# A decoder layer in fp32 on one core: conditioning loaded as columns, and the order of products and low parts in the opening

## The chip, the cores and the metric

The kernel runs on one core of one Trainium2 chip. The core has five engines with queues of their own: TensorE (PE; its weight loads are listed as PEld), VectorE (DVE), ScalarE (ACT), GpSimd (POOL) and SyncE (SP, which here only issues DMAs); POOL issues DMAs too. Both kinds of issue are served by the core's 16 DMA engines. The metric is the device time of one execution in microseconds, as the median of several runs.

## The reference

One layer over 2048 tokens of width 1024, all in float32. A conditioning vector `c` gives six modulation rows; shift and scale act on each sub-layer's input, the gate on its output.

```python
cond = jax.nn.silu(c)
mod = (cond @ w_ada[l] + b_ada[l])[:, None, :]
sh1, sc1, g1, sh2, sc2, g2 = jnp.split(mod, N_MOD, axis=-1)
h = x * (1.0 + sc1) + sh1
z = h @ w_in[l]
gate_b, gate_c, v_conv, v_pool = jnp.split(z, [CONV_CH, 2 * CONV_CH, 3 * CONV_CH], axis=-1)
y_conv = gate_b * _short_conv(gate_c * v_conv, conv_w[l])
y_pool = _multiscale_pool(v_pool, w_pool[l], pool_scale[l])
mix = jnp.concatenate([y_conv, y_pool], axis=-1) @ w_out[l]
x = _layer_norm(DEEPNORM_ALPHA * x + (1.0 + g1) * mix, ln1_g[l], ln1_b[l])
h = x * (1.0 + sc2) + sh2
f = jnp.square(jax.nn.relu(h @ w_mlp_in[l])) @ w_mlp_out[l]
x = _layer_norm(DEEPNORM_ALPHA * x + (1.0 + g2) * f, ln2_g[l], ln2_b[l])
```

## The kernel before

The tokens are processed in two blocks of 1024 (`T`), with channels on the 128 partitions, so that the width of 1024 is eight "inputs" of 128 channels (`KD` = 8). Every fp32 operand of a matmul is split into a high part, rounded to TensorE's one-pass fp32 format by a ScalarE copy or activation, and a low part, the difference, by a VectorE subtraction (`split`, lines 78 to 80). A product is three matmuls: high by high, weights' high by low, weights' low by high (`mm3`, lines 83 to 86). Larger matrix products are done in Strassen's manner with seven block products, whose block sums are made on VectorE beside them.

**Modulation.** `w_ada` is laid out so that a row of the modulation, 128 channels of one of the six vectors, is a tile of 128x1024 (`wada[f]`). VectorE multiplies the tile by `cond`, the silu of `c` repeated on all partitions, and sums along the row: one `scalar_tensor_tensor` with an accumulated output per channel group (line 168). A bias add for a few groups at once turns the accumulated columns into columns of `mod` (line 170). The small tile `vecs` (128x80) holds the biases and other per-channel constants as columns; 1 is added to the scale and gate biases on chip (line 148).

**The opening.** Lines 92 to 107: `c` is loaded in two halves, each broadcast to 128 partitions by SyncE, ScalarE takes the sigmoid, VectorE the product. `vecs` comes over POOL's queue. The first two rows of `wada` and half of input 0 are loaded in halves. TensorE runs `WARM` = 18 small matmuls on an identity (line 115). `ada_first` makes `mod` for input 0.

**The first group** (`first_group`, lines 324 to 354) computes the first quarter of the input projection's columns for block 0, with all eight PSUM banks open as accumulators, over the eight inputs `k` in turn. For each `k`: two rows of `wada`, a 128x512 slice of weights and the 128x1024 input are loaded through `in_turn`, which chains the DMAs' issue order on SyncE; the two row products and the bias give `mod` for this input; then the weights are split, and `make_a` makes the high part of x * scale + shift (line 193), the same in full precision in place (line 195 on ScalarE, or line 197 on VectorE for inputs 0 and 1), and the low part (line 198). 24 matmuls follow (line 353): 4 column tiles, 2 halves of the tokens, 3 products.

In this code an input's low parts are issued before the next input's two row products. The order of instructions on each engine is made by a scheduler from the program; `tc.issue_after(x)` makes what stands under it come after x on its engine. The engines run their queues in order and wait for each other through semaphores.

After the first group the other three quarters follow in `group_mm`, with convolution and pooling of the group just done on VectorE and ScalarE. Right after the first group, eight more rows of `wada` (the gate `g1`) are loaded and multiplied. `spread` (line 173) then transposes the eight columns of the gate into a row repeated on all partitions: eight transposes on TensorE of a column broadcast along the free dimension, into two PSUM banks, and two ScalarE copies. The output weights are multiplied by this row.

Of the kernel before, what the change touches and what calls it, by code (L numbers as in the profile page):

```python
# [27 lines left out]
WINDOWS = (2, 4, 8, 16)  # L28
HALO = 16
HALF_SUMS = (2, 2, 3, 3, 3, 3, 2, 0)  # L30
WARM = 18
WW = T + HALO

SC1, SH1 = 0, 1
G1 = 16
SC2, SH2 = 24, 25
G2 = 40
VB, VC, VP, VG, VBB = 0, 48, 60, 64, 72


@with_exitstack
def tile_hybrid_layer(ctx: ExitStack, tc: tile.TileContext, xT, x, c, wada, vec, win0, win,
                      wins, wpool, wout, wmix, w1, w2, rows, out):
    nc = tc.nc

# [26 lines left out]
    def t_ps():  # L72
        return mk(pp, [P, H], F32, "ps", 8)
# [4 lines left out]
    def split(src, hi, lo):  # L78
        high = nc.scalar.copy(hi, src)  # L79
        return high.ins, nc.vector.tensor_tensor(lo, src, hi.bitcast(F32), op=ALU.subtract).ins  # L80
# [8 lines left out]
        return nc.vector.tensor_tensor(out_, a, b_, op=op)  # L89


    vecs = cp.tile([P, 80], F32, name="vecs")
    cond = t_o(D)
    sig = t_o(D)
    halves = [slice(h * H, h * H + H) for h in range(2)]
    for hs in halves:
        nc.sync.dma_start(cond[:, hs], c[hs].partition_broadcast(P))
    first = [t_h(F32), t_h(F32)]
    nc.gpsimd.dma_start(vecs, vec)
    for i, f in enumerate((SC1, SH1)):  # L100
        for hs in halves:
            nc.sync.dma_start(first[i][:, hs], wada[f][:, hs])
    x0 = t_o()
    nc.sync.dma_start(x0[:, :H], xT[0, 0][:, :H])
    for hs in halves:
        nc.scalar.activation(sig[:, hs], cond[:, hs], AF.Sigmoid)
        nc.vector.tensor_tensor(cond[:, hs], cond[:, hs], sig[:, hs], op=ALU.mult)
# [29 lines left out]
    msum = tc.dram_tile([7, NG - 1, P, H], F32, name="msum")  # L137
    wosum = tc.dram_tile([2, 4, P, T], F32, name="wosum")

    def ada_first():  # L140
        for i in range(2):
            for h, hs in enumerate(halves):
                summed = nc.vector.scalar_tensor_tensor(
                    first[i][:, hs], first[i][:, hs], 1.0, cond[:, hs], op0=ALU.mult, op1=ALU.mult,
                    accum_out=part[:, 2 * h + i : 2 * h + i + 1])
        with tc.issue_after(summed.ins):
            for a, b, s in ((SC1, 16, 2), (G1, 24, 1), (SC2, 40, 2), (G2, 48, 1)):
                nc.vector.tensor_scalar_add(vecs[:, a:b:s], vecs[:, a:b:s], 1.0)
        nc.vector.tensor_tensor(part[:, 0:2], part[:, 0:2], vecs[:, 0:2], op=ALU.add)
        return nc.vector.tensor_tensor(mod[:, 0:2], part[:, 0:2], part[:, 2:4], op=ALU.add)  # L150

# [4 lines left out]
    def in_turn(dst, src):  # L156
        if before:
            with tc.issue_after(before.pop()):
                d = nc.sync.dma_start(dst, src)
        else:  # L160
            d = nc.sync.dma_start(dst, src)
        before.append(d.ins)

    def ada(f0, f1, load=nc.gpsimd.dma_start, tiles=lambda: t_h(F32)):
        for f in range(f0, f1):
            r = tiles()
            load(r, wada[f])
            nc.vector.scalar_tensor_tensor(r, r, 1.0, cond, op0=ALU.mult, op1=ALU.mult,  # L168
                                           accum_out=acc[:, f : f + 1])
        return nc.vector.tensor_tensor(mod[:, f0:f1], acc[:, f0:f1], vecs[:, f0:f1], op=ALU.add)  # L170


    def spread(dst, cols):
        for h, hs in enumerate(halves):
            ps = t_ps()
            for i in range(4):
                k = 4 * h + i
                nc.tensor.transpose(ps[:, i * P : i * P + P], cols[:, k : k + 1].to_broadcast([P, P]), ident)
            nc.scalar.copy(dst[:, hs], ps)

    def row(t, src):
        nc.sync.dma_start(t, src.partition_broadcast(P))
# [3 lines left out]
    lnb = cp.tile([P, KD], F32, name="lnb")  # L186


    def make_a(r, k, cs=slice(0, T), a=None, act=True):
        ahi, alo = a or (t_h(), t_h())  # L190
        sc = mod[:, 2 * k + SC1 : 2 * k + SC1 + 1]
        sh = mod[:, 2 * k + SH1 : 2 * k + SH1 + 1]
        nc.scalar.activation(ahi[:, cs], r[:, cs], AF.Identity, bias=sh, scale=sc)  # L193
        if act:
            nc.scalar.activation(r[:, cs], r[:, cs], AF.Identity, bias=sh, scale=sc)  # L195
        else:
            nc.vector.tensor_scalar(r[:, cs], r[:, cs], sc, sh, op0=ALU.mult, op1=ALU.add)  # L197
        nc.vector.tensor_tensor(alo[:, cs], r[:, cs], ahi[:, cs].bitcast(F32), op=ALU.subtract)  # L198
        return ahi, alo

    def load_m(src):
        r = t_r()
# [115 lines left out]
    def store_mixed(j, y, pt, u, v):  # L318
# [2 lines left out]
                                r.rearrange("p (a n) -> p a n", a=2))  # L321
        nc.gpsimd.dma_start(msum[6, j], v[:, :H])

    def first_group(A):
        ps = {}
        for k in range(KD):
            wr, wt = t_r(), t_w()
            if k == 0:
                done = ada_first()
                a, wcuts = x0, [slice(0, P), slice(P, H)]  # L330
                for cs in wcuts:
                    in_turn(wr[:, cs], win0[k][:, cs])
                in_turn(a[:, H:], xT[0, 0][:, H:])
            else:
                done = ada(2 * k, 2 * k + 2, in_turn)
                in_turn(wr[:, :H], win0[k])
                a, wcuts = t_o(), [slice(0, H)]
                in_turn(a, xT[0, k])
            opened.append(done.ins)
            with tc.issue_after(done.ins):  # L340
                pair = None
                for i in range(2):
                    for cs in wcuts[i : i + 1]:
                        split(wr[:, cs], wt[:, cs], wt[:, H + cs.start : H + cs.stop])
                    pair = make_a(a, k, halves[i], pair, k > 1)
                A.append(pair)
            for h, hs in enumerate(halves):
                for p in range(3):
                    for m in range(4):
                        if k == 0 and p == 0:  # L350
                            ps[m, h] = t_ps()
                        w = (H if p == 1 else 0) + m * P
                        nc.tensor.matmul(ps[m, h], wt[:, w : w + P], A[k][p // 2][:, hs],  # L353
                                         start=k == 0 and p == 0, stop=k == KD - 1 and p == 2)
        return ps
# [67 lines left out]
    def beside(j, m, g1):  # L423
        for what in plan.get((j, m), "").split():
            n = int(what[1:])
            if what[0] == "r":
                ada(n, n + 2)
            elif what[0] == "f":
                fold(n, g1)
            elif what[0] == "b":  # L430
                spread(g1, mod[:, G1 : G1 + KD])
# [576 lines left out]
    def down(b, F, g2, close):  # L1008
# [78 lines left out]
        for n, (i, hf) in enumerate(steps):  # L1087
            ops, _ = ready
            if n + 1 < len(steps):
                ready = operands(n + 1)  # L1090
            if b == 0 and n < 2:
                ada(G2 + 4 * n, G2 + 4 * n + 4, nc.sync.dma_start, lambda: t_o(D))
            if b == 0 and 2 <= n < 6:
                sum_x(n - 2, ready[1])
            if n == 5:
                next(later)
            if 5 <= n < 9:
                later.send(ready[1])
            if i in (4, 6) and hf == 1:
                rest[i] = saved(hi_ if i == 4 else lo_)  # L1100
                if i == 6:
                    close.turn()
            banks, new, then = table[i]
            matmuls(banks, ops, new, hf == 0, hf == 1, then, hf == 1 and i in (4, 5, 6))
            if b == 0 and n == 4:
                spread(g2, mod[:, G2 : G2 + KD])


    class Close:
# [98 lines left out]
def _lay(inputs):  # L1208
# [7 lines left out]
    def pairs(p, q):  # L1216
# [3 lines left out]
    bada = np.concatenate([pairs(vsc1, vsh1), vg1, pairs(vsc2, vsh2), vg2])  # L1220
    conv = a["conv_w"][0].reshape(3, NG, P).transpose(1, 0, 2).reshape(3 * NG, P)
    vec = np.concatenate([bada, conv, a["pool_scale"][0].reshape(NG, P),
                          a["ln1_g"][0].reshape(KD, P), a["ln1_b"][0].reshape(KD, P)]).T
    w = a["w_in"][0].reshape(KD, P, 4, NG, P)[:, :, [3, 1, 2, 0]]
    return {
        "xT": x.T.reshape(KD, P, NB, T).transpose(2, 0, 1, 3),
        "x": x,
        "c": a["c"][0],
        "wada": wada,
        "vec": vec,  # L1230
        "win0": w[:, :, :, 0].reshape(KD, P, 4 * P),
# [27 lines left out]
```

## Time and profile before

| | |
|---|---|
| median of 3 runs | 1751.06 us (1750.05 to 1752.57) |
| the profiled execution | 1750.36 us |
| its span, first to last instruction | 1748.4 us |
| granted TensorE clock | 0.998 |
| TensorE busy | 1730.1 us, 99% |
| VectorE busy | 1264.6 us, 72% |
| ScalarE busy | 861.4 us, 49% |
| POOL busy | 191.6 us, 11% |

A row of the timeline has the start in us from the start of the span, the busy time of the instructions merged in it, engine, source line, operation, output and inputs by the program's names with their shapes, the count, and in brackets how long the engine stood idle before and what released it. A tile's name has its pool's tag only (`h`, `o`, `w`, `r`), so that several uses share one. "SPq" rows are DMA issues on SyncE's queue. A group's row has busy time and mean duration, then the idle time before. A row of the waits has the engine, line and releaser, then the total in us, the count and the longest.

### The profile page before, as it was taken

The numbers are of one execution on the slowest core, as the hardware profiler recorded it, in microseconds if no ns is written. First come the engines' busy times: TensorE is split into PE (matmuls) and PEld (weight loads), VectorE is DVE, ScalarE is ACT, GpSimd is POOL, SyncE is SP. The second block draws the span as 40 slices with busy tenths as digits, with TensorE's granted clock in tenths as the row PEclk, the third lists the DMA queues.
The fourth block names the chain that finished last, engine by engine and source line by source line (L and its number), as shares of the span: only waits on it lengthen the run. The fifth ranks groups of instructions, "written<-read, shape, count | busy, mean of one in ns | idle before, by whom it ended". The sixth has DMA issues, their size and how long they took to land.

```text
span 1748.4 us, 21342 instructions
## 1 busy us (share of the span) xinstructions
PE 1730.1 (99%) x7692; PEld 1429.7 (82%) x7692; DVE 1264.6 (72%) x1624; ACT 861.4 (49%) x1168; POOL 191.6 (11%) x374
## 2 busy tenths in 40 slices
PE   8999999999999999999999999999999999999997
PEld 6788888888888888888888888888888888888886
DVE  6998697877777685669686789686565656465774
ACT  4423348555445555446573344775445564344452
POOL 0122211122232000000000000101000100000000
PEclk9999999999999999999999999999999999999999
DMA  9799868687888999778681366655433479577761
GB/s 368 302 338 348 315 231 293 253 317 296 324 323 304 351 412 339 281 267 292 211 271 69 119 222 213 219 198 208 145 132 145 154 266 375 193 252 263 256 238 61
DMA packets 137227, 444.22 MB, mean 254 GB/s; under 512 B 15633, under 2 KB 16401, under 8 KB 137121
## 3 DMA queue, kind: packets, MB, share of 16 engines
q1 hardware_dynamic: 95040, 293.38, 47.0%
q0 software_dynamic: 42080, 149.49, 22.5%
q8 instruction: 60, 0.98, 0.2%
q14 instruction: 47, 0.38, 0.1%
HBM read 308.06 MB, written 134.74 MB: 253 GB/s over the span
## 4 chain that ended last, share of the span: by engine, by line
PE 94%; DVE 2%; DMA 1%; ACT 1%; issue 0%; SPq 0%; DVEq 0%
PE ps L84 31%; PE ps L85 31%; PE ps L86 31%; DVE h L168 1%; PE ps L704 1%; DMA r<-in_w 1%; ACT h L193 1%; DVE h L198 1%; DMA o<-in_w 0%; DVE o L89 0%; PE ps L353 0%; DMA r<-in_win 0%; DVE w L80 0%; ACT o L195 0%; DVE o L197 0%
## 5 line engine op out<-in xcount | busy, mean ns | idle before, releaser
L84 PE MATMUL ps<-h,w 128*128 128x512 f32 x1312 | 510.2, 389 | 0.7 <-ACT o L916 0.4
L85 PE MATMUL ps<-h,w 128*128 128x512 f32 x1312 | 510.3, 389 | 0.0
L86 PE MATMUL ps<-h,w 128*128 128x512 f32 x1312 | 510.1, 389 | 0.0
L84 PE MATMUL ps<-h,h 128*128 128x512 f32 x1120 | 436.0, 389 | 0.0
L86 PE MATMUL ps<-h,h 128*128 128x512 f32 x1120 | 435.9, 389 | 0.0
L85 PE MATMUL ps<-h,h 128*128 128x512 f32 x1120 | 435.7, 389 | 0.0
L79 ACT CAST h<-r 128x1024 fp32r<-128x1024 f32 (+1 forms) x184 | 186.8, 1019 | 306.9 <-PE ps L85 204.8
L80 DVE TENSOR_TENSOR h<-r,h 128x1024 fp32r<-128x1024 f32 (+1 forms) x184 | 216.5, 1182 | 112.8 <-ACT h L79 112.4
L79 ACT CAST w<-r 128x1024 fp32r<-128x1024 f32 (+2 forms) x165 | 169.2, 1026 | 260.3 <-PE ps L85 241.2
L84 PEld LDWEIGHTS ps<-h,w 128*128 128x128 f32 x1312 | 246.0, 188 | 53.0 <-ACT o L916 0.8
L85 PEld LDWEIGHTS ps<-h,w 128*128 128x128 f32 x1312 | 246.3, 188 | 51.3 <-DVE h L80 0.5
L86 PEld LDWEIGHTS ps<-h,w 128*128 128x128 f32 x1312 | 246.3, 188 | 51.2
L80 DVE TENSOR_TENSOR w<-r,w 128x1024 fp32r<-128x1024 f32 (+2 forms) x165 | 196.3, 1190 | 109.1 <-ACT w L79 107.4
L86 PEld LDWEIGHTS ps<-h,h 128*128 128x128 f32 x1120 | 210.2, 188 | 43.7
L84 PEld LDWEIGHTS ps<-h,h 128*128 128x128 f32 x1120 | 210.2, 188 | 43.6
L85 PEld LDWEIGHTS ps<-h,h 128*128 128x128 f32 x1120 | 210.2, 188 | 43.4
L89 DVE TENSOR_TENSOR o<-o,o 128x1024 f32<-128x1024 f32 (+1 forms) x170 | 162.4, 959 | 60.3 <-DMA usum<-o 45.7
L89 DVE TENSOR_TENSOR o<-o,ps 128x512 f32<-128x512 f32 x156 | 105.6, 684 | 58.9 <-PE ps L86 58.1
L80 DVE TENSOR_TENSOR h<-w,h 128x1024 fp32r<-128x1024 f32 x112 | 136.7, 1221 | 3.6 <-ACT h L79 3.6
L79 ACT CAST h<-w 128x1024 fp32r<-128x1024 f32 x112 | 117.5, 1049 | 6.8 <-DMA w<-in_w 6.3
L929 POOL DMA_DIRECT2D usum<-o x112 | 59.7, 534 | 520.2 <-ACT o L926 233.5
L89 DVE TENSOR_TENSOR r<-r,r 128x1024 f32<-128x1024 f32 x60 | 73.4, 1223 | 18.7 <-DMA r<-in_w 16.0
(133 smaller groups left out, 1180.4 us busy)
## 6 DMA issues: line engine op xcount, KB each, us to landing
usum<-o POOLq DMA_DIRECT2D x112, 512.0 KB, 4.7
r<-usum SPq DMA_DIRECT2D x112, 512.0 KB, 4.9
w<-w2sum SPq DMA_DIRECT2D x64, 512.0 KB, 6.0
r<-in_w SPq DMA_DIRECT2D x60, 512.0 KB, 4.9
w<-in_w SPq DMA_DIRECT2D x48, 512.0 KB, 6.9
o<-in_w SPq DMA_DIRECT2D x72, 256.0 KB, 6.3
w2sum<-o POOLq DMA_DIRECT2D x64, 256.0 KB, 6.6
h<-in_wada SPq DMA_DIRECT2D x22, 512.0 KB, 9.1
```

Source lines behind the costliest of these rows:

```text
L79: high = nc.scalar.copy(hi, src)
L80: return high.ins, nc.vector.tensor_tensor(lo, src, hi.bitcast(F32), op=ALU.subtract).ins
L84: nc.tensor.matmul(ps, whi, xhi, start=first, stop=False, skip_group_check=goes_on)
L85: nc.tensor.matmul(ps, whi, xlo, start=False, stop=False, skip_group_check=goes_on)
L86: nc.tensor.matmul(ps, wlo, xhi, start=False, stop=last, skip_group_check=goes_on)
L89: return nc.vector.tensor_tensor(out_, a, b_, op=op)
L168: nc.vector.scalar_tensor_tensor(r, r, 1.0, cond, op0=ALU.mult, op1=ALU.mult, accum_out=acc[:, f : f + 1])
L193: nc.scalar.activation(ahi[:, cs], r[:, cs], AF.Identity, bias=sh, scale=sc)
L198: nc.vector.tensor_tensor(alo[:, cs], r[:, cs], ahi[:, cs].bitcast(F32), op=ALU.subtract)
L704: nc.tensor.transpose(ps[:, t * P : t * P + P], R[4 * h + t][:, k * P : k * P + P], ident)
L929: nc.gpsimd.dma_start(usum[g, i], r)
```

## The change

`c` becomes eight more columns of `vecs` (128x88), which is now the first load on SyncE's queue. The silu is taken on the 128x8 columns, the additions of 1 stand with it, and `spread` transposes them into two PSUM banks at once. The half-row products for input 0 read those banks; after input 0's high parts ScalarE copies them to `cond` for all later products. `WARM` is 7. In `first_group`, the loads of the next input are issued by the program before an input's low parts, and for inputs 1 to 6 the next input's first row product is placed ahead of the low parts and its second behind them. Input 0 keeps both products of input 1 behind its low parts. Full precision x * scale + shift is made on ScalarE for input 1 too; input 0 keeps VectorE for it.

```diff
-WARM = 18
+WARM = 7
...
-    vecs = cp.tile([P, 80], F32, name="vecs")
-    cond = t_o(D)
-    sig = t_o(D)
+    vecs = cp.tile([P, 88], F32, name="vecs")
+    nc.sync.dma_start(vecs, vec)
     halves = [slice(h * H, h * H + H) for h in range(2)]
-    for hs in halves:
-        nc.sync.dma_start(cond[:, hs], c[hs].partition_broadcast(P))
     first = [t_h(F32), t_h(F32)]
-    nc.gpsimd.dma_start(vecs, vec)
...
-    for hs in halves:
-        nc.scalar.activation(sig[:, hs], cond[:, hs], AF.Sigmoid)
-        nc.vector.tensor_tensor(cond[:, hs], cond[:, hs], sig[:, hs], op=ALU.mult)
+    silu = cp.tile([P, KD], F32, name="silu")
+    nc.scalar.activation(silu, vecs[:, VX : VX + KD], AF.Sigmoid)
+    tt(silu, silu, vecs[:, VX : VX + KD], ALU.mult)
+    for a, b, s in ((SC1, 16, 2), (G1, 24, 1), (SC2, 40, 2), (G2, 48, 1)):
+        nc.vector.tensor_scalar_add(vecs[:, a:b:s], vecs[:, a:b:s], 1.0)
...
+    def spread(cols):
+        banks = []
+        for h in range(2):
+            ps = t_ps()
+            for i in range(4):
+                k = 4 * h + i
+                nc.tensor.transpose(ps[:, i * P : i * P + P], cols[:, k : k + 1].to_broadcast([P, P]), ident)
+            banks.append(ps)
+        return banks
+
+    def row_of(dst, cols):
+        banks = spread(cols)
+        for h, hs in enumerate(halves):
+            nc.scalar.copy(dst[:, hs], banks[h])
+
+    cond_banks = spread(silu)
...
+    cond = t_o(D)
+
     def ada_first():
         for i in range(2):
             for h, hs in enumerate(halves):
-                summed = nc.vector.scalar_tensor_tensor(
-                    first[i][:, hs], first[i][:, hs], 1.0, cond[:, hs], op0=ALU.mult, op1=ALU.mult,
+                nc.vector.scalar_tensor_tensor(
+                    first[i][:, hs], first[i][:, hs], 1.0, cond_banks[h], op0=ALU.mult, op1=ALU.mult,
                     accum_out=part[:, 2 * h + i : 2 * h + i + 1])
-        with tc.issue_after(summed.ins):
-            for a, b, s in ((SC1, 16, 2), (G1, 24, 1), (SC2, 40, 2), (G2, 48, 1)):
-                nc.vector.tensor_scalar_add(vecs[:, a:b:s], vecs[:, a:b:s], 1.0)
...
+    def dot(f, r):
+        return nc.vector.scalar_tensor_tensor(r, r, 1.0, cond, op0=ALU.mult, op1=ALU.mult,
+                                              accum_out=acc[:, f : f + 1])
+
+    def biased(f0, f1):
+        return nc.vector.tensor_tensor(mod[:, f0:f1], acc[:, f0:f1], vecs[:, f0:f1], op=ALU.add)
...
+        wcuts = [slice(0, P), slice(P, H)], [slice(0, H)]
+        done = ada_first()
+        _, wr, a = loads(0)
+        for k in range(KD):
+            wt = t_w()
+            hi, lo = t_h(), t_h()
+            A.append((hi, lo))
             opened.append(done.ins)
             with tc.issue_after(done.ins):
-                pair = None
-                for i in range(2):
-                    for cs in wcuts[i : i + 1]:
-                        split(wr[:, cs], wt[:, cs], wt[:, H + cs.start : H + cs.stop])
-                    pair = make_a(a, k, halves[i], pair, k > 1)
-                A.append(pair)
+                for cs in wcuts[k > 0]:
+                    split(wr[:, cs], wt[:, cs], wt[:, H + cs.start : H + cs.stop])
+                for hs in halves:
+                    high = shifted(hi, a, k, hs)
+                    if k:
+                        shifted(a, a, k, hs)
+            if k + 1 < KD:
+                rows_, wr_n, a_n = loads(k + 1)
+            if k == 0:
+                with tc.issue_after(high.ins):
+                    for hs, bank in zip(halves, cond_banks):
+                        nc.scalar.copy(cond[:, hs], bank)
+            elif k + 1 < KD:
+                done = dot(2 * k + 2, rows_[0])
+            with tc.issue_after(done.ins):
+                for hs in halves:
+                    if k == 0:
+                        sc, sh = (mod[:, 2 * k + i : 2 * k + i + 1] for i in (SC1, SH1))
+                        nc.vector.tensor_scalar(a[:, hs], a[:, hs], sc, sh, op0=ALU.mult, op1=ALU.add)
+                    low = tt(lo[:, hs], a[:, hs], hi[:, hs].bitcast(F32), ALU.subtract)
+            if k + 1 < KD:
+                with tc.issue_after(low.ins):
+                    for i in range(k > 0, 2):
+                        dot(2 * k + 2 + i, rows_[i])
+                done = biased(2 * k + 2, 2 * k + 4)
+                wr, a = wr_n, a_n
```

`loads(k)` issues input k's two rows of `wada`, its weights and its input through `in_turn`, in the order of before. `shifted` is one ScalarE activation of x * scale + shift.

More of the change, by code (lines that the diff above doesn't have):

```diff
@@ L37, with tile_hybrid_layer @@
 G2 = 40
-VB, VC, VP, VG, VBB = 0, 48, 60, 64, 72
+VB, VC, VP, VG, VBB, VX = 0, 48, 60, 64, 72, 80
 @with_exitstack
-def tile_hybrid_layer(ctx: ExitStack, tc: tile.TileContext, xT, x, c, wada, vec, win0, win,
+def tile_hybrid_layer(ctx: ExitStack, tc: tile.TileContext, xT, x, wada, vec, win0, win,
                       wins, wpool, wout, wmix, w1, w2, rows, out):
@@ L167, in ada @@
             load(r, wada[f])
[L168 to L179, printed above, removed]
+            dot(f, r)
+        biased(f0, f1)
     def row(t, src):
@@ L186, in tile_hybrid_layer, with shifted @@
     lnb = cp.tile([P, KD], F32, name="lnb")
[L189 to L199, printed above, removed]
+    def shifted(dst, r, k, cs):
+        return nc.scalar.activation(dst[:, cs], r[:, cs], AF.Identity, bias=mod[:, 2 * k + SH1 : 2 * k + SH1 + 1],
+                                    scale=mod[:, 2 * k + SC1 : 2 * k + SC1 + 1])
     def load_m(src):
@@ L325, in first_group, with loads @@
         ps = {}
[L326 to L331, printed above, removed]
+        def loads(k):
+            rows_ = [t_h(F32) for _ in range(2 if k else 0)]
+            wr, a = t_r(), t_o() if k else x0
+            for i, r in enumerate(rows_):
+                in_turn(r, wada[2 * k + i])
+            if k:
+                in_turn(wr[:, :H], win0[k])
+                in_turn(a, xT[0, k])
+            else:
+                for cs in wcuts[0]:
@@ L332, in first_group @@
                     in_turn(wr[:, cs], win0[k][:, cs])
                 in_turn(a[:, H:], xT[0, 0][:, H:])
[L334 to L338, printed above, removed]
+            return rows_, wr, a
+        wcuts = [slice(0, P), slice(P, H)], [slice(0, H)]
[5 more added lines that the diff above has]
+            A.append((hi, lo))
@@ new lines, in first_group @@
+                for hs in halves:
+                    high = shifted(hi, a, k, hs)
+                    if k:
+                        shifted(a, a, k, hs)
[7 more added lines that the diff above has]
+                done = dot(2 * k + 2, rows_[0])
@@ L430, in beside @@
             elif what[0] == "b":
-                spread(g1, mod[:, G1 : G1 + KD])
+                row_of(g1, mod[:, G1 : G1 + KD])
             elif what[0] == "l":
@@ L1105, in down @@
             if b == 0 and n == 4:
-                spread(g2, mod[:, G2 : G2 + KD])
+                row_of(g2, mod[:, G2 : G2 + KD])
     class Close:
@@ L1222, in _lay @@
     vec = np.concatenate([bada, conv, a["pool_scale"][0].reshape(NG, P),
-                          a["ln1_g"][0].reshape(KD, P), a["ln1_b"][0].reshape(KD, P)]).T
+                          a["ln1_g"][0].reshape(KD, P), a["ln1_b"][0].reshape(KD, P),
+                          a["c"].reshape(KD, P)]).T
     w = a["w_in"][0].reshape(KD, P, 4, NG, P)[:, :, [3, 1, 2, 0]]
@@ L1227, in _lay @@
         "x": x,
-        "c": a["c"][0],
         "wada": wada,
```

## The prediction

> **What bounds the kernel now.** I read the page first, then who made TensorE wait, then the timeline of the opening, instruction by instruction.
>
> ```profile
> span 1748.4 us, 21342 instructions
> PE 1730.1 (99%) x7692; PEld 1429.7 (82%) x7692; DVE 1264.6 (72%) x1624; ACT 861.4 (49%) x1168; POOL 191.6 (11%) x374
> PE ps L353 <- ACT h L193: 4.0, 4, 2.1
> PE ps L115 <- POOL ident masks.py:199: 3.2, 1, 3.2
> 87.00:131.00 44.00, 44.00 (x196) 36.45 (x195) 40.95 (x73) 8.93 (x12) 9.39 (x16) 1.00 0.91 339
> ```
>
> TensorE is busy 99% of the span, and its only large waits are in the opening: for its first instruction and for L353, the first group's matmuls. A later window (span, PE, PEld, DVE, ACT, POOL, clock, DMA share, GB/s) has it busy 44.00 of 44.00 us while the DMA engines are at 0.91. So what the opening loses is lost for good, and what it gains should carry to the end.
>
> ```profile
> 0.74 0.86 SPq L97 DMA_DIRECT2D o<-in_c  x2
> 3.23 6.29 PE L115 MATMUL ps<-ident 128*128 128x128 f32 x36 [3.23 <-POOL ident masks.py:199]
> 4.41 0.63 ACT L106 ACTIVATE o<-o 128x512 f32<-128x512 f32 x1 [2.39 <-DMA o<-in_c]
> 6.78 0.69 DVE L107 TENSOR_TENSOR o<-o,o 128x512 f32<-128x512 f32 x1 [1.01 <-ACT o L106]
> 7.39 0.68 DVE L143 SCALAR_TENSOR_TENSOR h<-h,o 128x512 f32<-128x512 f32 x1
> 8.00 0.69 DVE L143 SCALAR_TENSOR_TENSOR h<-h,o 128x512 f32<-128x512 f32 x1
> 9.83 0.39 DVE L148 TENSOR_SCALAR vecs<-vecs 128x8 f32<-128x8 f32 x4
> 10.32 0.16 DVE L150 TENSOR_TENSOR mod<-small 128x2 f32<-128x2 f32 x1
> 10.38 0.51 ACT L79 CAST w<-r 128x384 fp32r<-128x384 f32 x1 [0.21 <-DMA r<-in_win]
> 10.79 1.52 ACT L193 ACTIVATE h<-o,mod 128x512 fp32r<-128x512 f32 x2
> 11.65 17.40 PE L353 MATMUL ps<-h,w 128*128 128x512 f32 x72 [2.13 <-ACT h L193]
> 16.42 0.16 DVE L170 TENSOR_TENSOR mod<-acc,vecs 128x2 f32<-128x2 f32 x1
> 17.49 5.33 PEld L353 LDWEIGHTS ps<-h,w 128*128 128x128 f32 x24 [0.50 <-ACT h L193]
> ```
>
> This is the start. The conditioning arrives broadcast, in two transfers that delay everything behind them: the second half is through sigmoid and product only at 7.4; then four half-row products (L143), the 1+ of the biases, the modulation `mod` of input 0 at 10.48, its high part on ScalarE from 10.79 (just after a weight cast that waited for its load), matmuls at 11.65. Input 1 reaches TensorE at 17.49.
>
> ```profile
> 28.43 0.16 DVE L170 TENSOR_TENSOR mod<-acc,vecs 128x2 f32<-128x2 f32 x1
> 28.51 0.69 DVE L80 TENSOR_TENSOR w<-r,w 128x512 fp32r<-128x512 f32 x1
> 28.63 1.52 ACT L193 ACTIVATE h<-o,mod 128x512 fp32r<-128x512 f32 x2 [2.74 <-DVE mod L170]
> 30.06 1.51 ACT L195 ACTIVATE o<-o,mod 128x512 f32<-128x512 f32 x2
> 30.89 1.40 DVE L198 TENSOR_TENSOR h<-o,h 128x512 fp32r<-128x512 f32 x2 [1.69 <-ACT o L195]
> 32.21 1.22 DVE L168 SCALAR_TENSOR_TENSOR h<-h,o 128x1024 f32<-128x1024 f32 x1
> 33.35 1.22 DVE L168 SCALAR_TENSOR_TENSOR h<-h,o 128x1024 f32<-128x1024 f32 x1
> 34.62 0.16 DVE L170 TENSOR_TENSOR mod<-acc,vecs 128x2 f32<-128x2 f32 x1
> 60.68 0.39 PE L84 MATMUL ps<-h,w 128*128 128x512 f32 x1
> 61.36 0.39 PE L84 MATMUL ps<-h,w 128*128 128x512 f32 x1
> ```
>
> This is the loop, one turn for each input. From `mod` to `mod` is 34.62 - 28.43 = 6.19 us: four passes on ScalarE, two low parts on VectorE (L198), two whole-row products for the next input (L168), bias. An input gives TensorE 24 matmuls; three start within 61.36 - 60.68 = 0.68 us, so 24 need 5.44. TensorE idles about 0.75 us per input because the VectorE-ScalarE loop is longer than its own work.
>
> **The loop.** In the changed kernel's instruction order, from input 1 on, the next input's first product stands between the weights' low part (L80) and the first low part. VectorE now idles 1.69 us there, and the product takes 1.22: it fits with some 0.4 to spare. Nothing is queued behind it that is needed sooner, for the low parts wait for ScalarE's second pair anyway. The chain loses one product, 33.35 - 32.21 = 1.14, and becomes 5.05: below TensorE's 5.44, which is the new period. From 17.49 to the next group's first matmul at 60.68 there are 43.19 us; seven turns at 5.44 are 38.1. **Gain 5.1.** If the product didn't fit and delayed the low parts by its whole length, this would be 0; were the loop still the bound at 5.6, it would be 4.0. More than 5.1 isn't to be had, since TensorE sets the end.
>
> Loads must keep this pace:
>
> ```profile
> 21.56 1.62 SPq L159 DMA_DIRECT2D h<-in_wada  x2
> 26.08 1.63 SPq L159 DMA_DIRECT2D h<-in_wada  x2
> 7.00:9.00 2.00, 2.00 (x18) 2.00 (x17) 2.00 (x6) 0.00 (x0) 0.00 (x0) 1.00 1.06 397
> 3.00:5.00 2.00, 1.76 (x8) 1.77 (x9) 0.02 (x1) 0.59 (x1) 0.18 (x1) 1.00 0.97 236
> ```
>
> SyncE's issues for successive inputs are 26.08 - 21.56 = 4.52 apart with the engines full, under 5.44; the changed kernel issues the same loads in the same order. Loads stay ahead.
>
> **The start.** Removed: two transfers of 256 KB of broadcast, two sigmoids and two products over 512 columns. While the broadcast ran, the engines moved 236 GB/s, later 397; 0.5 MB less is at least 1.3 us at 397. Added: `c` as eight columns of `vecs` (45 KB, moved from POOL's queue to the head of SyncE's), a sigmoid and a product on 128x8, eight transposes into two PSUM banks, two copies to `cond`; the 1+ moves ahead of it all; 18 warm-up matmuls become 7.
>
> ```profile
> o<-in_c SPq DMA_DIRECT2D x2, 256.0 KB, 4.3
> vecs<-in_vec POOLq DMA_DIRECT2D x1, 40.0 KB, 5.0
> DMA  0499999999999999999999999999999999999999
> 82.60 0.87 PE ps L178 x8
> L294 DVE TENSOR_TENSOR o<-o,ps 128x512 f32<-128x512 f32 x1 | 0.7, 683 | 0.0
> L143 DVE SCALAR_TENSOR_TENSOR h<-h,o 128x512 f32<-128x512 f32 x4 | 2.5, 686 | 0.0
> ```
>
> When `vecs` lands is not in the trace. The DMA slices (1.5 us each) show engines starting near 2.5, so 2.7 is the earliest; the first broadcast half, six times as large and at the same place, was used at 4.41; the old `vecs`, stuck behind it, took 5.0, which from 0.74 would be 5.7. I take 3.3, nearer the early end because only 45 KB move. Then the four 1+ (0.39) and a small product (0.16): 3.9. Eight transposes take 0.87 at 82 us; cold, going by 9 matmul rows in 1.77 us, 0.2 each: banks at 4.7 and 5.5. Four half products, 0.61 apart; reading one operand from PSUM costs nothing (683 against 686 ns): 4.8 to 7.2, and 0.4 for accumulator and sums, `mod` at 7.6. Their rows, 1 MB from 2.7 on at about 390 GB/s, land by 5.5, and input 0 and its weights by 7. So 10.48 becomes 7.6, and I take **2.8** for the start, a little off for semaphores. Bounds: 3.5 with `vecs` at 2.7; 1.3 if the loads come only 1.3 earlier; 0.6 with `vecs` at 5.7. From `mod` of input 0 to that of input 1 nothing gets longer: 6.10 us now, the same VectorE work after. The two copies (about 0.6 each) run on ScalarE behind input 0's high parts, before the cast of input 1's weights, which waits for its load now; without that cover they cost 1.2. The first matmuls into the two banks they free stand behind seventeen others (3.9 us), so TensorE doesn't wait.
>
> The warm-up is where I look for a loss. Matmul rows go from 9 in 3-5 us to 17 in 7-9 us: TensorE runs at half rate for some 4.5 us after it first works. In the changed kernel it first works at 3.9 and has 8 transposes and 14 rows, 4.4 us at 0.2; input 0 comes at about 8.7. If it is still at half rate there for 2 us, 1 is lost, of which 0.5 falls into the wait for input 1. I take 0.2, with 0 to 1. [...]
>
> **Sum.** 2.8 + 5.1 - 0.2 = 7.7 us. The profiled execution took 1750.36 (its span and 1.96 around it), 0.7 under the median of 1751.06; from the median, **1743.4**.
>
> **Does it carry?** The next thing that could be late is the gate row: eight more products, summed at
>
> ```profile
> 80.22 0.17 DVE L170 TENSOR_TENSOR mod<-acc,vecs 128x8 f32<-128x8 f32 x1
> 41.98 5.92 SPq L159 DMA_DIRECT2D h<-in_wada  x8
> ```
>
> and transposed on TensorE at 82.60 (above): 2.2 us of slack, 19.7 us after the first group's end. I laid the changed VectorE order from that end: the same eight products and convolution work, one weight split more before them and one fewer, 19.8 us; TensorE comes there 21.9 after it. Their eight loads are issued by 47.9 now and land some 9 us later (the broadcast's 1.3 us earlier in the changed kernel); they are needed up to 70. POOL has one load fewer ahead of its first store; that product, too, stands later on VectorE, and no matmul waits for it.
>
> **Rivals.** (1) Only the start gains: the early product delays the low parts and the turn stays 6.19. Against it: 1.69 idle against 1.22. 1751.1 - 2.8 + 0.2 = 1748.5. (2) Only the loop gains, because `vecs` lands as late as on POOL's queue (its 5.0 speaks for it; that it then queued behind 0.5 MB, against): 0.6 + 5.1, 1745.4. (3) The gain is given back at the gate row: DMA near full through 62 us and an earlier TensorE make the eight products late. Each us beyond 2 us of slack is lost; 4 late leaves 1747, all of it 1751. (4) Slower: with 7 warm-ups and gaps of about 0.5 us, TensorE stays at half rate through the first inputs. Each us of that loses half; from 16 us on (an input and a half) the loss passes 7.7 and the kernel is slower than before. Through four inputs, 24 matmuls each in 10.9 instead of 5.44, it loses 22: about 1765. Against it: the rate rose within 5 us of near-solid work before, and after the present gap of 2.1 us input 0's 24 matmuls were still through before 17.49, 5.8 us after the first.
>
> **How the numbers follow.** Forecast 0.76, (1) 0.06, (2) 0.08, (3) 0.06, (4) 0.04. What a measurement of this kernel can tell from no change is 0.2%, 3.5 us. The forecast, (2) and half of (3) are faster by more: 0.87. (1), at 2.6, and the other half of (3) are within it: 0.09. (4) is slower: 0.04. The forecast's own range is 1742 to 1745.5 (start 3.5 to 1.3, clock 0 to 1); up to 1747.6 takes in (2) and half of (3), and the lower end gets 0.5 more for the spread of the runs: 1741.5 to 1747.6.
>
> **What would show it.** First-group matmuls starting near 8.7 instead of 11.65; `mod` rows 5.4 apart or less; TensorE without a wait between inputs from input 1 on; the next group's first matmul near 53 instead of 60.68; the gate's transposes 21.9 after it. I am wrong if `vecs` lands past 4.4, if VectorE's low parts wait for the early product, if matmul rows of input 0 are 0.45 apart for long, or if a TensorE wait appears between 53 and 90.

## The result: slower by 1.06%

| | before | after |
|---|---|---|
| median | 1751.06 us (1750.05 to 1752.57) | 1770.05 us (1767.11 to 1771.85) |
| ratio, with 95% interval | | 1.0106 [1.0091, 1.0121] |
| profiled execution | 1750.36 us | 1771.85 us |
| its span | 1748.4 us | 1769.6 us |

The forecast was 1743.4, within 1741.5 to 1747.6. The time lies 22 us above the range, and on the other side of no change. The profiled execution of after is the slowest of its five runs, so the profiles differ by 21.5 us where the medians differ by 19.0.

The page of the changed kernel: span, busy times, and the chain that ended last by engine.

```profile
span 1769.6 us, 21316 instructions
PE 1752.8 (99%) x7678; PEld 1433.0 (81%) x7678; DVE 1264.6 (71%) x1621; ACT 862.1 (49%) x1171; POOL 191.1 (11%) x373
...
PE 92%; issue 2%; DMA 2%; DVE 2%; ACT 1%; SPq 0%; POOL 0%; DVEq 0%; ACTq 0%; POOLq 0%
```

TensorE is busy 99% of a longer span: 22.7 us more (1752.8 against 1730.1) with no more matmuls. VectorE, ScalarE and POOL are busy as long as they were, to within 1 us. So no wait took the place of another; TensorE itself works longer for the same matmuls. The groups of instructions, shapes kept apart (busy us, mean ns of one), say which, first after, then before:

```profile
L85 PE MATMUL ps<-h,w 128*128 128x512 f32 x1312 | 517.5, 395 | 0.0
L84 PE MATMUL ps<-h,w 128*128 128x512 f32 x1312 | 517.5, 395 | 1.2 <-DVE o L89 1.2
L84 PE MATMUL ps<-h,h 128*128 128x512 f32 x1120 | 436.0, 389 | 0.0
...
L387 PE MATMUL ps<-h,w 128*128 128x512 f32 x192 | 47.4, 410 | 2.6 <-ACT h L202 2.6
```

```profile
L85 PE MATMUL ps<-h,w 128*128 128x512 f32 x1312 | 510.3, 389 | 0.0
L84 PE MATMUL ps<-h,h 128*128 128x512 f32 x1120 | 436.0, 389 | 0.0
```

Matmuls with one operand in a tile `h` and the other in a tile `w` take 395 ns instead of 389; those with both in `h` take 389 in both kernels. That is no clock: the same instruction is slower or not by the tiles it reads. The windows (span, PE, PEld, DVE, ACT, POOL, clock, DMA share, GB/s) agree. Between 400 and 440 us the matmuls are of the first kind, between 640 and 680 of the second; after, then before:

```profile
400.00:440.00 40.00, 40.00 (x173) 32.17 (x172) 29.77 (x35) 18.48 (x22) 10.65 (x20) 1.00 0.81 302
640.00:680.00 40.00, 40.00 (x178) 33.11 (x178) 25.30 (x26) 20.46 (x21) 2.13 (x4) 1.00 1.01 397
```

```profile
400.00:440.00 40.00, 40.00 (x178) 33.13 (x177) 31.12 (x37) 18.36 (x22) 11.67 (x22) 1.00 0.85 324
```

In the same 40.00 us, with no idle time and the clock at 1.00, there are 173 matmuls instead of 178; in the other window 178. From start to start an `h,w` matmul takes 0.2328 us instead of 0.2268. Two rows of the timeline of after, twelve matmuls apart, show it: (60.63 - 57.84) / 12 = 0.2325.

```profile
57.84 0.39 PE L84 MATMUL ps<-h,w 128*128 128x512 f32 x1
...
60.63 0.39 PE L84 MATMUL ps<-h,w 128*128 128x512 f32 x1
```

Some 4110 such pairs at 6.0 ns make 24.6 us. Now the opening of after, by the timeline:

```profile
2.48 0.21 ACT L102 ACTIVATE silu<-vecs 128x8 f32<-128x8 f32 x1 [0.46 <-DMA vecs<-in_vec]
3.08 1.94 PE L118 MATMUL ps<-ident,silu 128*128 128x128 f32 x8 [3.08 <-DVE silu L89]
4.21 0.69 DVE L161 SCALAR_TENSOR_TENSOR h<-h,ps 128x512 f32<-128x512 f32 x1 [1.27 <-PE ps L118]
4.81 3.19 PE L131 MATMUL ps<-ident 128*128 128x128 f32 x14
7.23 0.69 DVE L161 SCALAR_TENSOR_TENSOR h<-h,ps 128x512 f32<-128x512 f32 x1 [2.32 <-DMA h<-in_wada]
8.83 0.30 ACT L79 CAST w<-r 128x128 fp32r<-128x128 f32 x1 [6.14 <-DMA r<-in_win]
9.24 0.16 DVE L165 TENSOR_TENSOR mod<-small 128x2 f32<-128x2 f32 x1
10.59 21.74 PE L387 MATMUL ps<-h,w 128*128 128x512 f32 x82 [2.58 <-ACT h L202]
...
20.38 0.16 DVE L184 TENSOR_TENSOR mod<-acc,vecs 128x2 f32<-128x2 f32 x1
22.84 1.40 DVE L89 TENSOR_TENSOR h<-o,h 128x512 fp32r<-128x512 f32 x2 [0.50 <-ACT o L202]
25.42 0.16 DVE L184 TENSOR_TENSOR mod<-acc,vecs 128x2 f32<-128x2 f32 x1
```

`vecs` lands at 2.48, earlier than forecast, but the second half-row product then waits 2.32 us for its row; `mod` is there at 9.40 (9.24 + 0.16) instead of 7.6, the first weights are cast only at 8.83, and the first matmul comes at 10.59 instead of 8.7. The loop does what was forecast: `mod` to `mod` is 25.42 - 20.38 = 5.04, and VectorE still idles 0.50 between the early product and the low parts.

Both kernels issue the same matmuls in the same order after the warm-up, so each can be set against itself. Start after minus start before, from the single records:

| point | after - before | what happened since the point above |
|---|---|---|
| first matmul of the first group | -1.1 us | the start gains 1.1 |
| first matmul of input 1 | +1.1 | 12 matmuls of input 0 some 427 ns apart, none before: 2.2 lost |
| first matmul of the next group (57.84 against 60.68) | -2.8 | -4.0: the loop gains 5.0, and gives back 1.0 to slower matmuls |
| end | +21.2 | some 23.4 from slower matmuls, and some 0.7 given back |

### The profile page after: what moved, and what is told of

Its sections match the earlier page's. It is cut to its first block, busy times and chain, and to the rows that moved or that the text cites. A ratio compares the mean times of both kernels' runs of the same rounds, so it can differ in the third digit from the quotient of the medians.

```text
span 1769.6 us, 21316 instructions
## 1 busy us (share of the span) xinstructions
PE 1752.8 (99%) x7678; PEld 1433.0 (81%) x7678; DVE 1264.6 (71%) x1621; ACT 862.1 (49%) x1171; POOL 191.1 (11%) x373
## 4 chain that ended last, share of the span: by engine, by line
PE 92%; issue 2%; DMA 2%; DVE 2%; ACT 1%; SPq 0%; POOL 0%; DVEq 0%; ACTq 0%; POOLq 0%
PE ps L84 30%; PE ps L85 30%; PE ps L86 30%; PE ps L387 3%; PE ps L738 1%; DMA w2sum<-o 0%; DVE h L80 0%; DVE o L89 0%; DMA usum<-o 0%; DMA r<-winsum 0%; DMA r<-in_xT 0%; DMA r<-in_win 0%; ACT h L587 0%; DMA r<-in_wins 0%; DMA r<-xsum 0%
## 5 line engine op out<-in xcount | busy, mean ns | idle before, releaser
L84 PE MATMUL ps<-h,w 128*128 128x512 f32 x1312 | 517.5, 395 | 1.2 <-DVE o L89 1.2
L86 PE MATMUL ps<-h,w 128*128 128x512 f32 x1312 | 517.7, 395 | 0.1
L85 PE MATMUL ps<-h,w 128*128 128x512 f32 x1312 | 517.5, 395 | 0.0
L84 PE MATMUL ps<-h,h 128*128 128x512 f32 x1120 | 436.0, 389 | 0.0
L86 PE MATMUL ps<-h,h 128*128 128x512 f32 x1120 | 435.9, 389 | 0.0
L79 ACT CAST w<-r 128x1024 fp32r<-128x1024 f32 (+2 forms) x165 | 168.9, 1024 | 296.4 <-PE ps L85 282.0
L84 PEld LDWEIGHTS ps<-h,w 128*128 128x128 f32 x1312 | 246.8, 188 | 60.0 <-DVE o L89 1.6
L86 PEld LDWEIGHTS ps<-h,w 128*128 128x128 f32 x1312 | 246.8, 188 | 59.0 <-DVE w L80 0.5
L80 DVE TENSOR_TENSOR h<-r,h 128x1024 fp32r<-128x1024 f32 (+1 forms) x184 | 216.0, 1179 | 107.9 <-ACT h L79 107.5
L80 DVE TENSOR_TENSOR w<-r,w 128x1024 fp32r<-128x1024 f32 (+2 forms) x165 | 196.2, 1189 | 126.2 <-ACT w L79 124.5
L86 PEld LDWEIGHTS ps<-h,h 128*128 128x128 f32 x1120 | 210.2, 188 | 43.8
L84 PEld LDWEIGHTS ps<-h,h 128*128 128x128 f32 x1120 | 210.3, 188 | 43.6
L80 DVE TENSOR_TENSOR h<-w,h 128x1024 fp32r<-128x1024 f32 x112 | 136.3, 1217 | 3.7 <-ACT h L79 3.7
```

The lines of the kernel that those rows point to most:

```text
L84: nc.tensor.matmul(ps, whi, xhi, start=first, stop=False, skip_group_check=goes_on)
L85: nc.tensor.matmul(ps, whi, xlo, start=False, stop=False, skip_group_check=goes_on)
L86: nc.tensor.matmul(ps, wlo, xhi, start=False, stop=last, skip_group_check=goes_on)
```

## The experiments

The theory for the 24.6 us: where the tiles lie in SBUF. Tiles of one tag get their place when the tag is first used. Before, `cond` and `sig` (tag `o`) came first, then `first` (tag `h`); the change allocates `first` ahead of any `o`. An `o` tile has 4160 bytes per partition (T + HALO numbers) and there are ten, 41600 bytes, which is no multiple of 256. They now lie between `h` and `w`. From the compiled programs, first byte of each tag in a partition:

```
kernel           order     h       o       w        w - h
before           o h r w   59776   18176   194944   135168 = 33 x 4096
after            h o r w   18240   132928  195008   176768 = 43 x 4096 + 640
before_h_first   h o r w   18176           194944   176768 = 43 x 4096 + 640
o_first          o h r w                            135168 = 33 x 4096
pad128           h o r w                            43 x 4096 + 768 = 691 x 256
pad64            h o r w                            43 x 4096 + 704 = 690 x 256 + 192
```

The rivals: something in the new order of the opening, or the shorter warm-up, slows the later matmuls. For what remains of the opening: the loop, the start, the warm-up, each alone.

**The place alone, in the changed kernel (o_first).** The tag `o` first again.

```diff
+    x0 = t_o()
     first = [t_h(F32), t_h(F32)]
...
-    x0 = t_o()
```

> The changed kernel with one allocation moved: the tile x0 (tag o) is made before the tiles of the first two rows (tag h), so that the tags stand in SBUF in the order o, h, r, w as before the change. Then w stands a multiple of 4096 bytes past h again (it is 640 more than one in the changed kernel). Theory of the addresses (weights and moving operand collide when they stand 640 bytes apart beyond multiples of 4096): the 4110 matmuls ps<-h,w take 227 ns from start to start again instead of 233, 24.6 us go, and the time is 1770 - 24.6 = 1745.5. Rival, the absolute place of w (448 past a multiple of 2048 instead of 384, which this edit leaves as it is): stays 1770. Rival, the PSUM banks taken in another turn, or the new order of instructions: stays 1770.

1747.28 us (1744.17 to 1751.33) against 1750.34: 0.9982 [0.9972, 0.9991]. A group of its matmuls, and its next group's first one:

```profile
L85 PE MATMUL ps<-h,w 128*128 128x512 f32 x1312 | 510.3, 389 | 0.0
```

```profile
55.66 0.39 PE L84 MATMUL ps<-h,w 128*128 128x512 f32 x1
```

One allocation moved, with the same work on each engine, is 22.8 us of medians, 1.8 less than was expected; the runs of this kernel spread over 7.2 us. The next group starts 5.0 us ahead of before.

**The place alone, in the kernel before (before_h_first).**

```diff
+    first = [t_h(F32), t_h(F32)]
     cond = t_o(D)
     sig = t_o(D)
...
-    first = [t_h(F32), t_h(F32)]
```

> The kernel before with the reverse edit and nothing of the change: the tiles of the first two rows are made before the conditioning's, so that the tags stand in the order h, o, r, w and w is 640 bytes more than a multiple of 4096 past h. Theory of the addresses: the matmuls ps<-h,w take 233 ns and the time is 1751 + 24.6 = 1775.6. Rivals (absolute place of w, PSUM banks, order of instructions): stays 1751.

1772.45 us (1772.13 to 1772.61) against 1750.34: 1.0125 [1.011, 1.014]. These 22.1 us are 2.5 fewer than the 24.6 expected. By the single records the slower matmuls cost 23.5 us behind the first group and nothing within it, where TensorE waits for the loop; the first group starts 0.4 us earlier, and two waits of TensorE near 341 and 353 us come out 1.0 us shorter. The old opening and the old order of products, with 395 ns:

```profile
L86 PE MATMUL ps<-h,w 128*128 128x512 f32 x1312 | 517.5, 395 | 0.0
```

The rivals fall: the loss needs nothing of the change but the order of allocation.

**The distance by itself (offsets).** Almost all of the layer is left out: 192 matmuls per source line, weights and moving operand at chosen distances in one tile.

```python
run(lambda *s, **k: mm(*s, **k), 0, 64)
...
run(lambda *s, **k: mm(*s, **k), 64, 64)
```

The first number is the moving operand's shift in bytes, the second the weights'.

> Matmuls alone, in the kernel's form (128x512 moving, 128x128 weights, high/low pattern of three), 192 for each distance between weights and moving operand, on the same data; almost all of the layer is left out. A line of the code for each distance: 0, 0, 16, 32, 64, 128, 192, 256, 320, 384, 448, 512, 640, 1024, 2048 bytes beyond multiples of 4096 with the moving operand at a multiple of 2048, then moving and weights both 64 past, moving alone 64 past, both 128 past, moving alone 128 past, both 32 past. Theory of the addresses: 389 ns mean duration at distance 0 and with both shifted together, about 395 at 640 and at 128; what 16 to 64 and 256, 512, 1024 and 2048 do is open, and tells the period of the collision. Rival, absolute place: both 64 past is slow, 640 (a multiple of 128) is not. Rival, neither: 389 on all lines.

Six of its groups; L72 is a distance of 0, L75 of 64, L76 of 128, L77 of 192, L78 of 256, and on L86 both operands are shifted by 64:

```profile
L72 PE MATMUL ps<-a 128*128 128x512 f32 x192 | 43.7, 389 | 0.0
L75 PE MATMUL ps<-a 128*128 128x512 f32 x192 | 45.0, 395 | 0.0
L76 PE MATMUL ps<-a 128*128 128x512 f32 x192 | 44.8, 395 | 0.0
L77 PE MATMUL ps<-a 128*128 128x512 f32 x192 | 44.1, 391 | 0.0
L78 PE MATMUL ps<-a 128*128 128x512 f32 x192 | 43.7, 389 | 0.0
L86 PE MATMUL ps<-a 128*128 128x512 f32 x192 | 43.7, 389 | 0.0
```

Of the other distances, 16, 512, 1024 and 2048 gave 389, 448 gave 391, and 32, 320, 384 and 640 gave 395. Shifting the moving operand alone gave 391 for 64 and 395 for 128; shifting both by 32 or 128 gave 389. So over the distances tried the pattern repeats every 256 bytes, and it is the distance between the two operands that counts, not the address of either.

**The distance in the changed kernel (pad128, pad64).** The order of allocation stays, with unused bytes between `o` and `w`.

```diff
     x0 = t_o()
+    big.tile([P, 32], F32, name="pad")
```

pad64 has 16 in place of 32.

> The changed kernel with its tags in its own order (h, o, r, w) and 128 unused bytes per partition between o and r, so that w stands 768 bytes past h beyond multiples of 4096, a multiple of 256. Theory of the addresses with a period of 256 (from the run of the distances): the matmuls ps<-h,w take 227 ns and the time is that of the kernel with the allocation moved, 1747. Rival, what counts is the order of the tags or the region of SBUF in which h lies: stays 1770.

> The same with 64 unused bytes: w stands 704 bytes past h, 192 beyond a multiple of 256. Theory of the addresses with a period of 256: the distance of 192 had 2.1 ns more for each matmul than 0 (44.1 against 43.7 us for 192), so 4110 matmuls lose 8.8 us and the time is 1747 + 9 = 1756. Rival, any distance off a multiple of 256 costs the same 6 ns: 1771.

pad128: 1746.67 us (1745.15 to 1749.12) against 1750.89, 0.9977 [0.9968, 0.9987]. pad64: 1754.69 (1752.27 to 1756.06), 1.0023 [1.0012, 1.0034]. 128 idle bytes are worth 23.4 us. 64 bytes, which leave 192 past a multiple of 256, are worth part of it; groups of pad64:

```profile
L85 PE MATMUL ps<-h,w 128*128 128x512 f32 x1312 | 515.1, 393 | 0.0
L86 PE MATMUL ps<-h,w 128*128 128x512 f32 x1312 | 510.1, 389 | 0.0
```

Two of the three products of `mm3` are slower there (L84 is 393 too) and the third isn't; by single records that is 8.9 us over the whole kernel.

**The loop alone (reorder_only).** The kernel before with the new `first_group`; conditioning, 18 warm-ups and places as before.

```diff
+            if 0 < k < KD - 1:
+                done = dot(2 * k + 2, rows_[0])
+            with tc.issue_after(done.ins):
+                for hs in halves:
...
+                    low = tt(lo[:, hs], a[:, hs], hi[:, hs].bitcast(F32), ALU.subtract)
```

> The kernel before with the new order in the first group alone (the next input's first product ahead of the low parts, full precision on ScalarE from input 1 on); conditioning, warm-up and places in SBUF as before. Theory of the loop: the chain from input to input is shorter than TensorE's 5.44 us, 5.1 us go in the opening, about 1 comes back at the stall near 350 us: 1750.3 - 4.1 = 1746.2. Rival, the loop's gain needs the early start: 1749 or more.

1745.65 us (1745.34 to 1746.35): 0.9972 [0.9962, 0.9982], 5.2 us under the kernel before on the same chip (1750.89). Its next group starts at 55.65 instead of 60.68:

```profile
55.65 0.39 PE L84 MATMUL ps<-h,w 128*128 128x512 f32 x1
```

**The columns alone (columns_only, columns_mended).** o_first with 18 warm-ups and the old `first_group`.

```diff
+                if k == 0:
                     for hs, bank in zip(halves, cond_banks):
                         nc.scalar.copy(cond[:, hs], bank)
```

> The changed kernel with the first group's order of before, 18 warm-up matmuls, and the tags in the order o, h, r, w: of the change only the conditioning as columns is left. Theory of the start: input 0's matmuls begin 1.5 us earlier, the loop of 6.19 us an input carries this on: 1750.3 - 1.5 = 1748.8. Rival, the loads of the first inputs set the pace of the loop when it starts earlier: no gain, 1750.3.

1750.04 us (1748.42 to 1752.42): 0.9997 [0.9987, 1.0006]. Its timeline says that it was no clean measure of the columns:

```profile
9.61 1.07 ACT L362 COPY o<-ps 128x512 f32<-128x512 f32 x2
10.57 1.53 ACT L205 ACTIVATE h<-o,mod 128x512 fp32r<-128x512 f32 x2
11.44 6.93 PE L369 MATMUL ps<-h,w 128*128 128x512 f32 x22 [1.79 <-ACT h L205]
```

The two bank copies stand ahead of input 0's high parts on ScalarE and delay them by 10.57 - 9.61 = 0.96 us. TensorE then waits 1.79 us (its warm-up had ended at 9.65, 36 rows in 4.70 us or 0.13 each, where those of after stood 0.21 apart and the last ones of before 0.11: at full rate by then), and by the single records its matmuls 7 to 13 after that stand 427 ns apart, at half rate; the granted clock from 12 to 14 us was 0.71. columns_mended puts the copies behind the high parts, as the change does:

```diff
-                if k == 0:
+            if k == 0:
+                with tc.issue_after(made[-1].ins):
                     for hs, bank in zip(halves, cond_banks):
```

> As the run with the conditioning as columns alone (18 warm-up matmuls, order of the first group as before, tags o, h, r, w), but with ScalarE's two copies of the banks behind input 0's high parts, as the changed kernel has them; in the run before they stood ahead and cost 1 us. Theory of the start: input 0's matmuls begin some 1.3 us earlier than before the change, which the loop carries on: 1750.5 - 1.3 = 1749.2. Rival, nothing is left of it at the end: 1750.5.

1749.14 us (1747.58 to 1749.87) against 1750.74: 0.999 [0.998, 0.9999]. The columns are worth 1.6 us here, just more than the interval. The 18 warm-ups take something off that: input 0's high part starts at 9.04 and its first matmul comes at 10.41, where with 14 warm-ups (next experiment) it follows the high part's start by 0.86, about half a us sooner.

**The warm-up (o_first_warm18, o_first_warm14).** o_first with `WARM` 18, then 14.

```diff
-WARM = 7
+WARM = 18
```

> The changed kernel with the allocation moved as above and 18 warm-up matmuls instead of 7. In the changed kernel the first 12 matmuls of input 0 start 427 ns apart, half rate. Theory of the clock: with 18 the warm-up reaches 10 us without a gap, the first group's matmuls start at full rate, and the time is 2 us under that of the same kernel with 7 (about 1743.4). [...]

> The changed kernel with x0 allocated first and 14 warm-up matmuls. With 18 they ran until 10.3 us and input 0's matmuls stood behind them for half a us; with 7 they ended 2.4 us before them and the rate fell. Theory of the clock: 14 end about when input 0's high part is ready, near 9.5, with no gap over half a us: 1744.3 to 1744.8, with a spread of the runs under 2 us as with 18. Rival, four fewer already let the rate stay or fall to half: a spread of 4 us and a median of 1746 or more.

With 18: 1744.81 us (1743.55 to 1744.93) against 1750.34, 0.9966 [0.9953, 0.9979]. With 14: 1744.28 (1744.1 to 1745.87), also 0.9966 [0.9952, 0.9979]: 6.5 us under the kernel before on the same chip (1750.74), and the lowest median of the versions tried, though it can't be told from that with 18. The runs with 18 and with 14 spread over 1.4 and 1.8 us; those of the kernels with 7 warm-ups spread over 3.8 (pad64) to 7.2 us (o_first). The end of the warm-up and the first matmuls, with 18, then with 14 (and from its groups, the first group's):

```profile
4.95 5.34 PE L131 MATMUL ps<-ident 128*128 128x128 f32 x36
10.05 8.29 PE L387 MATMUL ps<-h,w 128*128 128x512 f32 x35
```

```profile
4.99 3.80 PE L131 MATMUL ps<-ident 128*128 128x128 f32 x28
9.54 8.63 PE L387 MATMUL ps<-h,w 128*128 128x512 f32 x35 [0.75 <-ACT h L202]
...
53.59 0.39 PE L84 MATMUL ps<-h,w 128*128 128x512 f32 x1
```

```profile
L387 PE MATMUL ps<-h,w 128*128 128x512 f32 x192 | 44.2, 391 | 0.8 <-ACT h L202 0.8
```

18 warm-ups (36 rows) cover the whole wait and last too long by about half a us; 14 leave a gap of 0.75. In neither profile is a matmul of the first group at half rate: the first group's mean with 14 is 391 ns, where it is 410 in after. The next group starts at 53.59.

## Why the prediction was wrong

**The step that failed** is the one on which the sum rests: "what it gains should carry to the end", with TensorE's own work, "three start within 61.36 - 60.68 = 0.68 us", taken over as unchanged. The sum has no term for a change of that pace: it was put at nothing, without a reason. TensorE did set the end, as the first views said, and for that reason 6.0 ns more on each of 4110 matmuls came out in full: 24.6 us, three times all that the change could gain. The prediction went through the instructions that the diff adds, removes and moves. It did not ask what the diff does to the places of the tiles, though the two allocations of tag `o` that stood ahead of `first` leave that place in plain sight. None of the four rivals was of this kind: rival 4 has a slower kernel, but by half rate in the first inputs, which cost 2.2 us here. Undoing the place alone (o_first), or the distance alone (pad128), brings back 22.8 and 23.4 us of medians; doing it alone (before_h_first) costs 22.1 against the kernel before on the same chip.

**The loop** was right: forecast 5.1. From input 1 to the next group's first matmul after gains 4.0, or 5.0 with the slower matmuls taken out; alone (reorder_only) it is worth 5.2 in the medians. The early product fitted with 0.50 to spare, where 0.4 was forecast, and rival 1 falls.

**The start** had the right sign and the wrong size: 2.8 forecast, 1.1 in after, 1.3 in o_first (10.38 against 11.65), 2.1 with 14 warm-ups (9.54). The part that failed is "Their rows, 1 MB from 2.7 on at about 390 GB/s, land by 5.5, and input 0 and its weights by 7": in after a half row was still awaited until 7.23 and the first weights until 8.83. The changed kernel and its variants with the same loads started input 0 at 9.54 to 10.59 in one profiled execution each (10.08 in pad128, 10.32 in pad64), so part of the difference between the three starts is scatter. The low rate of the first microseconds had been put down to the broadcast. The window from 2 to 8 us, before, after, and with 14 warm-ups:

```profile
2.00:8.00 6.00, 4.76 (x24) 4.77 (x25) 2.17 (x6) 1.28 (x3) 1.17 (x21) 1.00 0.92 277
```

```profile
2.00:8.00 6.00, 4.92 (x22) 4.66 (x22) 1.93 (x10) 0.23 (x2) 0.00 (x0) 1.00 0.86 272
```

```profile
2.00:8.00 6.00, 4.74 (x31) 4.77 (x32) 2.92 (x12) 0.43 (x3) 0.00 (x0) 1.00 0.92 300
```

The last number of a row is GB/s: the broadcast is gone and the engines move 272 to 300, as against 277 with it. So in these rows less to load helps only by its bytes; that the rate rises for it doesn't show. Why it is low there stays open.

**The warm-up** was where the loss was looked for, and there was one: 0.2 forecast, 0 to 1 allowed, 2.2 in after. The warm-up ended at 8.0, TensorE idled 2.58 us instead of the 2.1 of before, and the first 12 matmuls stood some 427 ns apart. Full rate came near 15.8, by the spacing of the matmuls. In windows from 12 to 14 us, after, then before:

```profile
12.00:14.00 2.00, 2.00 (x6) 1.58 (x5) 2.00 (x3) 0.19 (x1) 0.00 (x0) 1.00 0.92 339
```

```profile
12.00:14.00 2.00, 2.00 (x10) 1.65 (x9) 1.93 (x4) 0.31 (x1) 0.00 (x0) 1.00 1.03 408
```

Six matmuls instead of ten, though both rows give the granted clock as 1.00: over so short a stretch the count of matmuls told the rate, and the clock's column did not. The gap was that long because input 0 was late; whether 7 warm-ups would have done for a start at 8.7 was not tried. With seven more this loss is gone. It is also not the same in each execution: with the same seven, input 0 started at half rate in after and pad128, and at full rate for its first six matmuls in o_first. (The prediction's 9 and 17 matmul rows are the counts of the weight loads; TensorE's own in its two windows are 8 and 18, and nothing hangs on the difference.)

**The carry past the gate row** held, and rival 3 falls. The bias sum and the transposes in after:

```profile
76.98 0.16 DVE L184 TENSOR_TENSOR mod<-acc,vecs 128x8 f32<-128x8 f32 x1
80.23 1.03 PE L118 MATMUL ps<-ident,mod 128*128 128x128 f32 x8
```

There are 3.1 us of slack, where before had 2.2. A small part is given back elsewhere. The waits of TensorE on VectorE's sums, after and before:

```profile
PE ps L84 <- DVE o L89: 1.2, 1, 1.2
```

```profile
PE ps L84 <- DVE o L89: 0.3, 1, 0.3
```

It is one wait, near 356 us in after. In o_first it is 1.6, but with 14 warm-ups, where TensorE comes earliest, it is 0.3 as before, and a wait of 0.7 for a low part of the weights (L80) has come up elsewhere. From the next group's first matmul to the end o_first loses 1.1 us of its gain, and the version with 14 warm-ups 0.7; which wait takes it differs.

Put together with the measured sizes: start -1.1, warm-up +2.2, loop -5.0, slower matmuls +24.6, given back some 0.7: +21.4 on 1750.36, which is 1771.8. The profiled execution took 1771.85. With the places and the warm-up mended (o_first_warm14) the change is worth 6.5 us of the 7.7 forecast.

## What to carry to other kernels

An edit that adds, removes or reorders allocations is a change of addresses: before costing its instructions, compare where the operands of the bounding engine's hot instructions lie in both compiled programs, here modulo 256 bytes between a matmul's weights and its moving operand. When a profile shows the same count of instructions with more busy time, compare the mean duration group by group, by the tiles that they read; one group that moves while its neighbour doesn't is no clock. And where one part of a change spoils the whole, undo that part alone before the change is dropped: here one line moved and seven more warm-up matmuls make a kernel that is 1.06% slower into one that is 0.34% faster.

## What the runs showed of the hardware that had not been expected

- A matmul of 128x128 weights and 128x512 fp32 values took 389 ns, and followed its predecessor at 227 ns, with weights and moving operand a multiple of 256 bytes apart, or 16 past it; 395 and 233 at 32, 64 or 128 past it (45.0, 45.0 and 44.8 us for 192 in offsets, against 43.7); 391 on average at 192 past it in the lone matmuls. So the pace depends on where the two operands lie to each other, by 2.6% in after (233 against 227 ns). Why is not shown.
- TensorE was at half rate, its matmuls 427 ns apart, after a warm-up of 4.9 us (from 3.08 to 8.0 in after) and a gap of 2.58, and its rate fell after a gap of only 1.79 in columns_only. The length of the gap alone doesn't decide: in before no matmul of input 0 is at half rate behind a gap of 2.13. From 12 to 14 us the granted clock was 0.50 in o_first, pad128 and pad64, behind gaps of 2.36, 2.98 and 2.51, with 6, 6 and 7 matmuls, and 1.00 with 14 and 18 warm-ups, behind a gap of 0.75 and none, with 10 each; in after it is given as 1.00 with 6.
- From 2 to 8 us the DMA engines moved 277 GB/s with 0.5 MB of broadcast at the head of the queue, and 272 and 300 without it. What holds them back at first was not tried.
